# A decoder layer in split fp32: where the weight subtraction and the normalised tiles stand in program order

## The chip, the cores and the metric

The kernel runs on one core of one Trainium2 chip. The number that counts is the device time of one execution in microseconds (us). Before the change it is 1643.07 us, the median of 3 runs (1643.04 to 1643.13).

## The reference

One decoder layer is applied to 256 prompt tokens and 8 x 4 sample tokens, all in fp32. Cut to what matters here:

```python
mod = (silu(c) @ w_ada + b_ada)              # six shifts, scales and gates per conditioning row
h = rms(x, g_mix) * (1 + sc_m) + sh_m
proj = h @ w_in                              # 2048 x 9216, split into b, c, hc, u, v, ga, gb
ya = b * shortconv(c * hc)
yb = gelu(u) * (causal_mix(rms(gelu(v), g_v)) + b_sg)
x = x + gt_m * ((sigmoid(ga) * (ya @ w_pa) + sigmoid(gb) * (yb @ w_pb)) @ w_out)
h2 = rms(x, g_ffn) * (1 + sc_f) + sh_f
x = x + gt_f * ((silu(gate) * up) @ w_ffn_out)   # gate, up = h2 @ w_ffn_in
return rms(x, g_final), conv states, normalised v rows
```

The 288 tokens are the free axis everywhere; features lie on the 128 partitions.

## The kernel before

**Products.** Each 128x128 weight tile is used against 288 tokens once per pass. To keep fp32 accuracy, weights and activations are each split into a high part (rounded to the matmul type fp32r) and a low remainder. One tile product is then a *triple* of matmuls (L238 to L240): high x high, high x low, low x high.

**The split of weights.** A block of weights (1 MB or less) is brought by DMA into one of 7 `raw` buffers. `Blk.split` (L467) takes it in segments of 4 tiles (128x512): ScalarE (ACT in the profile) casts it to `hi` (L479), VectorE (DVE) subtracts to get `lo` (L485). `hi` and `lo` have 4 buffers each, so a cast waits until TensorE (PE) has done the last triple on the segment four before.

**The paced part.** In roughly the first 280 us the order on ACT, DVE and the DMA queue is the order in which the Python code issues the work (PE's order is so throughout). After each triple `feed()` (L247) issues the next segment when no more than `LEAD` (11) tiles are split ahead; cast and subtraction are issued together. When an accumulation in PSUM (`pm`, 4 banks) is complete, its sink copies or adds it into SBUF, an *eviction* (L712 on ACT or L714 on DVE for the unit wA; L735 for the next ones), and `evicted()` (L256) runs one waiting *job*.

**Units.** wA multiplies all 72 column tiles by the first 2 of the 16 k tiles (9 blocks of 16 triples; an eviction after every 2 triples). wB, wX and wC do k tiles 2 to 7 (an eviction after 3 or 6 triples). wD does k tiles 8 to 15 and lies behind the paced part. Blocks of the conditioning product (`ada`: aA, aC, aD, aE) stand between them. wA begins with x not yet normalised (`xe`), so that the sum of squares (`squares1`, L565) can be made meanwhile: its pieces are squares on ACT (L576) and sums on DVE (L579).

**The root.** `root()` (L987) puts three steps into a list of late work: the sums over features (L598) after 16 triples, `diagonal` (L208: L211 and L217 on DVE) 5 triples later, `norm1` (L602) 3 triples later; it multiplies by the diagonal on PE (L223) and copies the result to `rb` (L605).

**The jobs.** `make_h1(k0, k1)` makes the modulated input tiles k0 to k1 in four stages, one tile one stage further at each eviction: `scaled` (L302 on DVE, needs `rb`), `affine` (L617 on ACT, L618 and L619 on DVE, needs the conditioning), `high` (L624 on ACT) and `low` (L630 on DVE). Tiles 2 to 4 are made during wA's block 7, tiles 5 to 7 during wB's last two blocks, each just before the unit that reads them.

Then comes `free` (L995): the remaining jobs are run, the pacing ends, and a scheduler orders ACT, DVE and the DMA queue from there.

Of the kernel before, what the change touches and what calls it, by code (L numbers as in the profile page):

```python
# [22 lines left out]
DFF = 5632  # L23
SLOTS = 92
RAW = 7
LEAD = 11
SEG = 4
SPB = 4
GK = 0.7978845608028654
# [59 lines left out]
def _body(tc, nc, d, pc, pw, pslot, ptmp, pps):  # L89
# [9 lines left out]
    def slot(dt=F32, shape=(P, T)):  # L99
        return pslot.tile(list(shape), dt, tag="s", name=nm("s"), padded_shape=[P, TU])  # L100

    def tmp(n=T):
        return ptmp.tile([P, n], F32, tag="t", name=nm("t"), padded_shape=[P, TU])
# [63 lines left out]
    def token_rstd(ss, n, half=False, gaps=None):  # L167
        got = {}
        V.tensor_tensor(ss.acc, ss.acc, ss.last, ALU.add)

        def fold():
            got["ps"] = psmisc()
            square_sum(got["ps"], ss.acc, True, True)

        steps = [fold, lambda: roots(got, n, half)]
        for f, gap in zip(steps, gaps or (0, 0, 0)):
            if gaps:
                later(f, gap)
            else:
                f()  # L180
        return got
# [26 lines left out]
    def diagonal(got):  # L208
        r = got["r"]
        g = got["diag"] = tmp()  # L210
        V.tensor_tensor(  # L211
            g[:, :TP].rearrange("p (b t) -> p b t", b=2),
            ident.unsqueeze(1).to_broadcast([P, 2, P]),
            r[:, 0:2].unsqueeze(2).to_broadcast([P, 2, P]),
            ALU.mult,
        )
        V.tensor_scalar(g[:, TP:], ident[:, 96:], r[:, 2:3], None, ALU.mult)  # L217
# [26 lines left out]
            feed()  # L244
        return lh

    def feed():  # L247
        while S["feed"] and S["given"] - S["used"] <= LEAD:
            b = S["feed"][0]
            n = len(b.parts or [])  # L250
            b.split(1)
            S["given"] += len(b.parts) - n
            if len(b.parts) == b.nk * b.nm:
                S["feed"].pop(0)
# [10 lines left out]
    jobs = []  # L265
# [3 lines left out]
    def later(f, gap=0):  # L269
        if not pending:  # L270
            since[0] = 0
        pending.append((f, gap))
# [14 lines left out]
    def sam(ap):  # L287
        return ap.rearrange("p (b s) -> p b s", s=NS)

    def bc4(ap):  # L290
        return ap.unsqueeze(2).to_broadcast([P, NB, NS])
# [8 lines left out]
    def normed(kt, rb):  # L300
        t = slot()
        V.tensor_tensor(t, x[:, kt, :], rb, ALU.mult)  # L302
        return t

    def modulate(ks, get, gm, sh0, out):
        hs, his = {}, {}

        def affine(k, t):
            h = tmp()
            hi = slot(F32R)  # L310
            A.activation(
                h[:, :TP], t[:, :TP], AF.Identity, bias=mod[:, sh0 + k, 0:1], scale=gm[:, k, 0:1]
            )
            V.tensor_tensor(sam(h[:, TP:]), sam(t[:, TP:]), bc4(gm[:, k, 1:]), ALU.mult)
            V.tensor_tensor(sam(h[:, TP:]), sam(h[:, TP:]), bc4(mod[:, sh0 + k, 1:]), ALU.add)
            A.copy(hi, h)
            hs[k], his[k] = h, hi

        def finish_(k):
            lo = slot(F32R)  # L320
            V.tensor_tensor(lo, hs[k], his[k].bitcast(F32), ALU.subtract)
            out[k] = (his[k], lo)

        ts = {}
        n = len(ks)
        for i in range(n + 2):
            if i < n:
                ts[i] = get(ks[i])
            if 1 <= i <= n:
                affine(ks[i - 1], ts.pop(i - 1))  # L330
            if i >= 2:
                finish_(ks[i - 2])
# [25 lines left out]
    class Step:  # L358
        defer = False
        raw = None  # L360
        parts = None
# [187 lines left out]
    def ada(name):  # L549
        u = units[name]  # L550
        return [Ada(u, b) for b in range(16 // u[3])]


    S = {}
# [5 lines left out]
    def warm(n, out=None):  # L560
        out = idle if out is None else out
        for _ in range(n):
            PE.matmul(out[:, :T], wb[:, :P], wb, start=True, stop=True)
# [38 lines left out]
    def norm1():  # L602
# [3 lines left out]

        make_h1(0, 2)

    def make_h1(k0, k1):
        made = {}  # L610

        def scaled(k):
            made[k] = normed(k, S["rb1"])

        def affine(k):
            t, h = made[k], tmp()
            A.activation(h[:, :TP], t[:, :TP], AF.Identity, bias=mod[:, k, 0:1], scale=gm1[:, k, 0:1])  # L617
            V.tensor_tensor(sam(h[:, TP:]), sam(t[:, TP:]), bc4(gm1[:, k, 1:]), ALU.mult)  # L618
            V.tensor_tensor(sam(h[:, TP:]), sam(h[:, TP:]), bc4(mod[:, k, 1:]), ALU.add)  # L619
            made[k] = h  # L620

        def high(k):
            hi = slot(F32R)
            A.copy(hi, made[k])  # L624
            made[k] = (made[k], hi)

        def low(k):
            h, hi = made.pop(k)
            lo = slot(F32R)
            V.tensor_tensor(lo, h, hi.bitcast(F32), ALU.subtract)  # L630
            h1[k] = (hi, lo)

        def job(i):
            def f():
                for at, part in enumerate((scaled, affine, high, low)):
                    if k0 <= i - at < k1:
                        part(i - at)

            return f

        jobs.extend(job(i) for i in range(k0, k1 + 3))

    def do_jobs():
        while jobs:
            jobs.pop(0)()
# [38 lines left out]
    def gm_of(k0, k1):  # L684
        V.scalar_tensor_tensor(
            gm1[:, k0:k1, :],
            mod[:, 16 + k0 : 16 + k1, :],
            1.0,
            gmix[:, k0:k1].unsqueeze(2).to_broadcast([P, k1 - k0, NC]),
            ALU.add,  # L690
            ALU.mult,
        )

    def mk_h1(k0, k1):
        def f():
            gm_of(k0, k1)
            if S.get("paced") is not None:
                return make_h1(k0, k1)
            modulate(range(k0, k1), lambda k: normed(k, S["rb1"]), gm1, 0, h1)

        return Do(f)

    part, raws = {}, {}
# [30 lines left out]
    def sinkB(m, ps):  # L734
        return V.tensor_tensor(part[m], ps[:, :T], part[m], ALU.add)  # L735
# [158 lines left out]

    def rstd2():
        S["r2"] = token_rstd(S["acc2"], D, gaps=(9, 0))
        later(lambda: diagonal(S["r2"]), 4)

    def norm2():
        ps = rstd_bcast(S["r2"])  # L900
# [3 lines left out]
    def mk_h2(k0, k1):  # L904
        def f():
            modulate(range(k0, k1), lambda k: normed(k, S["rb2"]), gm2, 48, h2)

        return Do(f)
# [53 lines left out]
    def at(main, plan):  # L962
        out, n = [], 0
        for s in main:
            out.append(s)
            if isinstance(s, Blk):
                n += 1
                out += plan.pop(n, [])
        assert not plan
        return out  # L970

    aA, aC, aD, aE = ada("aA"), ada("aC"), ada("aD"), ada("aE")
# [3 lines left out]
    wB = [Blk("wB", i, rh1, lambda m, ps: sinkB(LATER + m, ps)) for i in range((72 - LATER) // 4)]  # L976
# [7 lines left out]
    steps = [Do(lambda: warm(24)), aA[0], Do(lambda: warm(8)), aA[1], Do(lambda: warm(6)), aA[2], Do(lambda: warm(6)), aA[3]]  # L984
    steps += [Do(mk_xe), Do(lambda: warm(7))]

    def root():  # L987
        later(sums1, 16)
        later(lambda: diagonal(S["r1"]), 5)
        later(norm1, 3)  # L990

    plan = {2: [Do(root, None)], 5: aC[:4], 7: aC[4:] + [mk_h1(2, 5)]}
    steps += at(wA, plan)
    steps += at(wB, {2: aD[:4], 4: aD[4:] + [mk_h1(5, 8)]})
    free = Do(lambda: None, None)  # L995
    steps += at(wX + wC, {3: aE[:4], 8: aE[4:8], 13: aE[8:12], 18: aE[12:] + [free, mk_h1(8, 12), mk_h1(12, 16)]})

# [21 lines left out]
    def ffin(q):  # L1019
        fi = [Blk("fi", i - 4, h2.__getitem__, lambda j, ps: sink_fi(j + 4, ps)) for i in range(max(4, 22 * q), 22 * q + 22)]  # L1020
        return fi
# [3 lines left out]

    fk = [KBlk("fk", i, xg.__getitem__, sink_fk) for i in range(4)]
    nxt = ffin(1)
    steps += [fk[0], Do(norm2, 3), mk_h2(0, 6), fk[1], mk_h2(6, 11), fk[2], mk_h2(11, 16), fk[3]]
    steps += at(ffin(0) + nxt[:2], {2: a5[:4], 6: a5[4:8], 10: a5[8:12], 14: a5[12:]})
    for q in range(3):  # L1030
        steps += ffout(q) + nxt[2:]
# [26 lines left out]
    for s in steps:  # L1058
        if s is free:
            do_jobs()  # L1060
            S["paced"] = None
            head.close()
        if isinstance(s, Do):
            if pending and s.gap is not None:
                later(s.run, s.gap)
            else:
                s.run()
            continue
        i = pos[id(s)]
        if i + AHEAD < len(stream):  # L1070
            stream[i + AHEAD].load()
        while (
            nxt < len(blks)
            and blks[nxt].raw is not None
            and nxt <= cur + 1
            and S["paced"] is None
        ):
            blks[nxt].split()
            nxt += 1
        s.run()  # L1080
        if isinstance(s, Blk):
            cur += 1
            nxt = max(nxt, cur)
# [109 lines left out]
```

## Time and profile before

| what | value |
|---|---|
| median of 3 runs | 1643.07 us |
| the profiled execution | 1643.07 us |
| its span, first to last instruction | 1641.3 us |
| mean granted TensorE clock | 0.998 |
| PE busy | 1625.7 us, 99% of the span |
| DVE busy, ACT busy | 1011.1 us, 738.7 us |

The span is 1.8 us shorter than the time of the same execution. PE is TensorE's matmuls and PEld its weight loads, which run ahead of the matmuls. In a row of the timeline stand the start in us from the span's start, the busy time in us, the engine, the line, the operation, its output and inputs, and in brackets how long the engine was idle before it and what ended that.

### The profile page before, as it was taken

To read this page: it belongs to the slowest core of one execution; us is meant where nothing else is said; L and a number is where in the kernel's file an instruction comes from. 1 tells how busy PE (TensorE), PEld (TensorE's weight loads), DVE (VectorE), ACT (ScalarE), POOL (GpSimd) and SP (SyncE) were. 2 spreads that over 40 slices of the span, in tenths; PEclk is the share of its full clock that TensorE was granted. 3 is DMA by queue.
4 is the path that set the end of the run, shared out by engine and by line. 5 is a ranking of instruction groups with operands and counts; after the bars stand their busy time and mean duration, and the time that the engine had idled before them with its cause. 6 is when DMAs were issued, how large, how long until landed. Compare 5 with 4: busy or idle time off the path is not lost.

```text
span 1641.3 us, 31007 instructions
## 1 busy us (share of the span) xinstructions
PE 1625.7 (99%) x12360; PEld 1550.4 (94%) x12360; DVE 1011.1 (62%) x2162; ACT 738.7 (45%) x1359; POOL 21.7 (1%) x67
## 2 busy tenths in 40 slices
PE   9999999999999999999999999999999999999997
PEld 6889899998998999999998999999999999999997
DVE  5567687877755567667844555555555555555565
ACT  4543344643444334456743434444444444444453
POOL 0000000000000000011000000000000000000000
PEclk9999999999999999999999999999999999999999
DMA  9777775766786767744576546443464434644341
GB/s 366 288 282 288 299 271 201 268 257 261 292 315 257 274 245 289 272 177 154 195 310 249 208 168 206 176 159 122 161 211 175 156 131 159 220 158 169 111 157 58
DMA packets 59425, 357.56 MB, mean 218 GB/s; under 512 B 6640, under 2 KB 9616, under 8 KB 28560
## 3 DMA queue, kind: packets, MB, share of 16 engines
q1 hardware_dynamic: 58992, 355.38, 58.5%
q8 instruction: 96, 1.57, 0.4%
q14 instruction: 49, 0.40, 0.1%
q10 hardware_dynamic: 288, 0.21, 0.0%
HBM read 352.47 MB, written 3.09 MB: 217 GB/s over the span
## 4 chain that ended last, share of the span: by engine, by line
PE 96%; DVE 1%; DMA 1%; ACT 1%; issue 0%; DVEq 0%; ACTq 0%; SPq 0%
PE pm L238 30%; PE pm L239 30%; PE pm L240 30%; PE ada L394 5%; DMA raw<-in_wA 1%; DMA raw<-in_aA 1%; DVE lo L485 0%; ACT hi L479 0%; DVE x L957 0%; DMA ct<-in_c 0%; DVE s L714 0%; PE px L190 0%; PE px L795 0%; PE px L836 0%; DVE s L302 0%
## 5 line engine op out<-in xcount | busy, mean ns | idle before, releaser
L238 PE MATMUL pm<-s,hi 128*128 128x288 f32 (+1 forms) x3760 | 1112.9, 296 | 1.6 <-DVE s L714 1.3
L239 PE MATMUL pm<-s,hi 128*128 128x288 f32 (+1 forms) x3760 | 1110.3, 295 | 1.1 <-DVE s L630 0.7
L240 PE MATMUL pm<-s,lo 128*128 128x288 f32 (+1 forms) x3760 | 1109.7, 295 | 0.2 <-DVE lo L677 0.2
L485 DVE TENSOR_TENSOR lo<-raw,hi 128x512 fp32r<-128x512 f32 (+1 forms) x959 | 654.2, 682 | 497.7 <-ACT hi L479 483.7
L479 ACT CAST hi<-raw 128x512 fp32r<-128x512 f32 (+1 forms) x960 | 588.0, 613 | 801.1 <-PE pm L239 787.1
L238 PEld LDWEIGHTS pm<-s,hi 128*128 128x128 f32 x3760 | 707.1, 188 | 21.9 <-issue 15.9
L239 PEld LDWEIGHTS pm<-s,hi 128*128 128x128 f32 x3760 | 706.8, 188 | 2.2 <-DVE s L630 0.9
L240 PEld LDWEIGHTS pm<-s,lo 128*128 128x128 f32 x3760 | 706.4, 188 | 0.4 <-DVE lo L677 0.4
L394 PE MATMUL ada<-raw,cs 128*32 128x512 f32 (+2 forms) x832 | 88.9, 563 | 1.5 <-DMA raw<-in_aA 1.1
L394 PEld LDWEIGHTS ada<-raw,cs 128*32 128x32 f32 x832 | 23.8, 109 | 48.5 <-issue 43.0
L743 DVE TENSOR_TENSOR s<-pm,s 128x288 f32<-128x288 f32 x72 | 32.9, 457 | 15.9 <-PE pm L240 15.8
L338 DVE SCALAR_TENSOR_TENSOR x<-pm,mod,x 128x256 f32<-128x256 f32 x80 | 38.0, 475 | 2.7 <-PE pm L240 2.7
L297 DVE TENSOR_TENSOR s<-t,s 128x288 fp32r<-128x288 f32 (+1 forms) x76 | 34.7, 459 | 5.9 <-ACT s L295 5.9
L295 ACT CAST s<-t 128x288 fp32r<-128x288 f32 (+1 forms) x76 | 32.6, 433 | 12.4 <-DVE t L775 5.5
L735 DVE TENSOR_TENSOR s<-pm,s 128x288 f32<-128x288 f32 x56 | 25.2, 453 | 7.9 <-PE pm L240 7.8
L922 DVE SCALAR_TENSOR_TENSOR t<-t,pm 128x288 f32<-128x288 f32 x42 | 19.1, 454 | 16.5 <-PE pm L240 16.5
L344 DVE TENSOR_TENSOR t<-pm,mod 128x32 f32<-128x32 f32 x80 | 15.3, 191 | 18.6 <-PE pm L240 18.6
L712 ACT COPY s<-pm 128x298 f32<-128x298 f32 (+1 forms) x42 | 16.9, 403 | 19.7 <-PE pm L240 19.7
L159 ACT ACTIVATE t<-x 128x288 f32<-128x288 f32 (+2 forms) x31 | 13.5, 437 | 20.5 <-DVE x L347 17.4
L720 DVE SCALAR_TENSOR_TENSOR s<-pm,s 128x256 f32<-128x256 f32 x40 | 19.2, 481 | 5.0 <-PE pm L240 5.0
L164 DVE TENSOR_TENSOR acc<-acc,t 128x288 f32<-128x288 f32 x34 | 15.5, 456 | 8.2 <-ACT t L159 8.2
L204 POOL TENSOR_TENSOR r<-e,mhalf 128x3 f32<-128x3 f32 x4 | 4.2, 1040 | 1159.5 <-DVE e L203 1159.5
(134 smaller groups left out, 460.6 us busy)
## 6 DMA issues: line engine op xcount, KB each, us to landing
raw<-in_fi SPq DMA_DIRECT2D x84, 1024.0 KB, 4.8
raw<-in_a SPq DMA_DIRECT2D x64, 1024.0 KB, 9.5
raw<-in_f SPq DMA_DIRECT2D x64, 704.0 KB, 4.1
raw<-in_wD SPq DMA_DIRECT2D x36, 1024.0 KB, 4.9
raw<-in_wC SPq DMA_DIRECT2D x24, 768.0 KB, 4.6
raw<-in_aE SPq DMA_DIRECT2D x16, 1024.0 KB, 10.0
raw<-in_wo SPq DMA_DIRECT2D x16, 1024.0 KB, 4.9
raw<-in_pa SPq DMA_DIRECT2D x8, 1024.0 KB, 5.7
```

Of the source, the lines that this page charges most:

```text
L238: PE.matmul(out, wh, ah, start=first, stop=False)
L239: PE.matmul(out, wh, al, start=False, stop=False)
L240: lh = PE.matmul(out, wl, ah, start=False, stop=last)
L295: A.copy(hi, a)
L297: V.tensor_tensor(lo, a, hi.bitcast(F32), ALU.subtract)
L338: V.scalar_tensor_tensor(x[:, m, :TP], ps[:, :TP], mod[:, gt0 + m, 0:1], x[:, m, :TP], ALU.mult, ALU.add)
L394: PE.matmul(acc[32 * j : 32 * j + 32, :w], cs[:, kt, :], self.raw[:, o : o + w], start=(kt < ks), stop=(kt >= 16 - ks), tile_position=(0, ...
L479: A.copy(hi, self.raw[:, s * 128 : e * 128])
L485: sub()
L720: V.scalar_tensor_tensor(t[:, :TP], ps[:, :TP], t[:, T : T + 1], t[:, :TP], ALU.add, ALU.add)
L735: return V.tensor_tensor(part[m], ps[:, :T], part[m], ALU.add)
L743: V.tensor_tensor(a, ps[:, :T], a, ALU.add)
```

## The change

The subtraction of a segment is issued two triples after its cast instead of together with it (`lows`, `LAG`), and a segment is fed when 12 instead of 11 tiles are ahead, so a cast is issued one triple earlier and its subtraction one triple later than before. The first stage of the jobs (`scaled`) of tiles 2 to 4 and 5 to 7 is issued one block (wA) or one block (wB) earlier by `pre_h1`; `make_h1` then has three stages. The steps of the root stand 6 and 4 triples apart instead of 5 and 3. At the second norm the two gaps change from 4 and 3 to 3 and 4.

```diff
-LEAD = 11
+LEAD = 12
+LAG = 2
...
-    def feed():
+    lows = []
+
+    def feed(force=False):
+        while lows and (force or S["used"] >= lows[0][0]):
+            lows.pop(0)[1]()
         while S["feed"] and S["given"] - S["used"] <= LEAD:
             b = S["feed"][0]
             n = len(b.parts or [])
-            b.split(1)
+            low = []
+            b.split(1, low)
+            lows.append((S["used"] + LAG, low[0]))
...
+    made = {}
+
+    def pre_h1(k0, k1):
+        def scaled(k):
+            def f():
+                made[k] = normed(k, S["rb1"])
+
+            return f
+
+        return Do(lambda: jobs.extend(scaled(k) for k in range(k0, k1)), None)
+
     def make_h1(k0, k1):
-        made = {}
...
-                for at, part in enumerate((scaled, affine, high, low)):
+                for at, part in enumerate(parts):
...
-        jobs.extend(job(i) for i in range(k0, k1 + 3))
+        parts = (affine, high, low) if k0 in made or jobs else (scaled, affine, high, low)
+        jobs.extend(job(i) for i in range(k0, k1 + len(parts) - 1))
...
-        later(lambda: diagonal(S["r2"]), 4)
+        later(lambda: diagonal(S["r2"]), 3)
...
-        later(lambda: diagonal(S["r1"]), 5)
-        later(norm1, 3)
+        later(lambda: diagonal(S["r1"]), 6)
+        later(norm1, 4)
 
-    plan = {2: [Do(root, None)], 5: aC[:4], 7: aC[4:] + [mk_h1(2, 5)]}
+    plan = {2: [Do(root, None)], 5: aC[:4], 6: [pre_h1(2, 5)], 7: aC[4:] + [mk_h1(2, 5)]}
     steps += at(wA, plan)
-    steps += at(wB, {2: aD[:4], 4: aD[4:] + [mk_h1(5, 8)]})
+    steps += at(wB, {2: aD[:4], 3: [pre_h1(5, 8)], 4: aD[4:] + [mk_h1(5, 8)]})
...
-    steps += [fk[0], Do(norm2, 3), mk_h2(0, 6), fk[1], mk_h2(6, 11), fk[2], mk_h2(11, 16), fk[3]]
+    steps += [fk[0], Do(norm2, 4), mk_h2(0, 6), fk[1], mk_h2(6, 11), fk[2], mk_h2(11, 16), fk[3]]
...
             do_jobs()
+            feed(True)
             S["paced"] = None
```

PE executes the same instructions in the same order but for one place, and the DMA queue's order stays. In the changed kernel the same statements have other line numbers: the triple is L239 to L241, the cast L486, the subtraction L252, wA's evictions L730 (ACT) and L732 (DVE), `scaled` L309, `affine` L634 to L636, `high` L641, `low` L647.

The place on PE is the root's product with the diagonal (`px<-t,ones`), in wA's fourth block. Before:

```order
L240 MATMUL pm_119_597<-s_21_236,lo_94_510 128x298
L238 MATMUL pm_119_597<-s_23_242,hi_93_508 128x298
L239 MATMUL pm_119_597<-s_24_244,hi_93_508 128x298
L240 MATMUL pm_119_597<-s_23_242,lo_94_510 128x298
L223 MATMUL px_121_606<-t_117_589,ones_78 128x288
L238 MATMUL pm_123_610<-s_21_236,hi_99_531 128x298
```

And now, with the same names:

```order
L241 MATMUL pm_119_597<-s_23_242,lo_92_503 128x298
L239 MATMUL pm_123_609<-s_21_236,hi_97_524 128x298
L240 MATMUL pm_123_609<-s_22_238,hi_97_524 128x298
L241 MATMUL pm_123_609<-s_21_236,lo_98_526 128x298
L239 MATMUL pm_123_609<-s_23_242,hi_97_524 128x298
L240 MATMUL pm_123_609<-s_24_244,hi_97_524 128x298
L241 MATMUL pm_123_609<-s_23_242,lo_98_526 128x298
L224 MATMUL px_125_619<-t_118_594,ones_78 128x288
```

The product moved behind two more triples. On ACT, at the same place before (`hi` casts of weights from `raw`, evictions `s<-pm`, and the copy of the root `rb<-px`):

```order
L479 CAST hi_109_563<-raw_11_154 128x512
L712 COPY s_113_579<-pm_112_572 128x298
L479 CAST hi_115_585<-raw_13_174 128x512
L712 COPY s_118_595<-pm_114_581 128x298
L712 COPY s_120_604<-pm_119_597 128x298
L605 COPY rb_122_608<-px_121_606 128x288
L479 CAST hi_124_614<-raw_13_174 128x512
L712 COPY s_129_632<-pm_128_625 128x298
```

And now:

```order
L486 CAST hi_103_547<-raw_11_154 128x512
L730 COPY s_105_550<-pm_102_540 128x298
L486 CAST hi_113_579<-raw_13_174 128x512
L730 COPY s_115_582<-pm_112_572 128x298
L730 COPY s_117_592<-pm_116_584 128x298
L486 CAST hi_120_604<-raw_13_174 128x512
L730 COPY s_122_607<-pm_119_597 128x298
L612 COPY rb_126_621<-px_125_619 128x288
```

Each cast moved ahead of the eviction of the accumulation that ends with the triple that frees its buffer, and one cast ahead of the copy of the root. In wA the subtractions on DVE keep their places among the evictions.

On DVE in wA's block 7, from the third `scaled` tile to the eviction of the block's seventh accumulation, before:

```order
L302 TENSOR_TENSOR s_245_1056<-x_77,rb_122_608 128x288
L618 TENSOR_TENSOR t_246_1058<-s_241_1041,gm1_89 128x32
L619 TENSOR_TENSOR t_246_1058<-t_246_1058,mod_88 128x32
L485 TENSOR_TENSOR lo_250_1070<-raw_173_789,hi_249_1068 128x512
L618 TENSOR_TENSOR t_252_1077<-s_245_1056,gm1_89 128x32
L619 TENSOR_TENSOR t_252_1077<-t_252_1077,mod_88 128x32
L630 TENSOR_TENSOR s_254_1083<-t_242_1043,s_247_1062 128x288
L630 TENSOR_TENSOR s_258_1096<-t_246_1058,s_253_1081 128x288
L485 TENSOR_TENSOR lo_261_1104<-raw_173_789,hi_260_1102 128x512
L714 COPY s_262_1109<-pm_259_1098 128x288
L630 TENSOR_TENSOR s_263_1111<-t_252_1077,s_257_1094 128x288
```

And now, to the eviction of the same accumulation (`pm_262`):

```order
L635 TENSOR_TENSOR t_244_1049<-s_208_908,gm1_89 128x32
L636 TENSOR_TENSOR t_244_1049<-t_244_1049,mod_88 128x32
L635 TENSOR_TENSOR t_250_1067<-s_211_920,gm1_89 128x32
L636 TENSOR_TENSOR t_250_1067<-t_250_1067,mod_88 128x32
L647 TENSOR_TENSOR s_252_1073<-t_241_1035,s_245_1053 128x288
L252 TENSOR_TENSOR lo_248_1064<-raw_175_792,hi_247_1062 128x512
L647 TENSOR_TENSOR s_256_1087<-t_244_1049,s_251_1071 128x288
L647 TENSOR_TENSOR s_261_1101<-t_250_1067,s_255_1085 128x288
L252 TENSOR_TENSOR lo_259_1098<-raw_175_792,hi_258_1096 128x512
L732 COPY s_263_1111<-pm_262_1103 128x288
L252 TENSOR_TENSOR lo_266_1122<-raw_175_792,hi_265_1120 128x512
```

The `scaled` tiles are no longer in this stretch (they stand in block 6), and all three `low` stand ahead of that eviction. In wB's last two blocks the same holds on DVE: three `scaled` move from there to the block before, and the third `low` stands one eviction earlier.

## The prediction

> **What bounds the kernel now.** I read the page first: the span, and who is busy in it.
>
> ```profile
> span 1641.3 us, 31007 instructions
> PE 1625.7 (99%) x12360; PEld 1550.4 (94%) x12360; DVE 1011.1 (62%) x2162; ACT 738.7 (45%) x1359; POOL 21.7 (1%) x67
> ```
>
> TensorE sets the time (the page's chain is PE for 96%), and the change neither adds nor removes a matmul. So it can only win what PE waits. The span lies 1.8 us below the execution's 1643.07 us, which is also the median, so what is won in the span comes off 1643.07. Next the windows and the waits of the weight loads, since the order changes only before about 290 us:
>
> ```profile
> 20.00:45.00 25.00, 24.36 (x170) 23.00 (x169) 20.32 (x38) 16.58 (x32) 1.40 (x1) 1.00 0.99 379
> 45.00:132.00 87.00, 85.00 (x674) 76.46 (x672) 56.40 (x129) 43.33 (x92) 0.00 (x0) 1.00 0.75 288
> 132.00:280.00 148.00, 148.00 (x1132) 136.81 (x1131) 111.44 (x288) 55.14 (x92) 0.00 (x0) 1.00 0.71 266
> ...
> PEld pm L238 <- DVE s L714: 2.5, 5, 1.1
> PEld pm L239 <- DVE s L630: 0.9, 1, 0.9
> ```
>
> The columns behind the length are PE, PEld, DVE, ACT and POOL busy, the granted clock (1.00) and the DMA share. PE has no gap at all from 132 to 280; the two wait rows (20 to 132 us), and a third stop at the root, hold nearly all there is to win. The timeline of PE shows the four large stops, each with the matmul before it:
>
> ```profile
> 43.74 0.30 PE L240 MATMUL pm<-s,lo 128*128 128x298 f32 x1
> 44.63 0.75 PE L223 MATMUL px<-t,ones 128*128 128x288 f32 x2 [0.60 <-DVE t L217]
> ...
> 51.65 0.30 PE L240 MATMUL pm<-s,lo 128*128 128x298 f32 x1
> 52.40 0.40 PE L238 MATMUL pm<-s,hi 128*128 128x298 f32 x1 [0.45 <-DVE s L714]
> 52.64 0.30 PE L239 MATMUL pm<-s,hi 128*128 128x298 f32 x1
> 52.77 0.30 PE L240 MATMUL pm<-s,lo 128*128 128x298 f32 x1
> ...
> 83.05 0.29 PE L240 MATMUL pm<-s,lo 128*128 128x288 f32 x1
> 84.22 0.40 PE L238 MATMUL pm<-s,hi 128*128 128x288 f32 x1 [0.88 <-DVE s L714]
> ...
> 125.09 0.30 PE L238 MATMUL pm<-s,hi 128*128 128x288 f32 x1
> 126.05 0.40 PE L239 MATMUL pm<-s,hi 128*128 128x288 f32 x1 [0.67 <-DVE s L630]
> ```
>
> Undisturbed matmuls start 0.13 us apart (52.64 to 52.77), three of them, a triple, take 0.40. After a stop the second start comes 0.24 later (52.40 to 52.64): 0.10 more is lost. Counted from start to start, the stops cost A: 44.63-43.74-0.13 = 0.76 (a matmul of another kind follows, so no 0.10); B: 0.62+0.10 = 0.72; C: 1.04+0.10 = 1.14; D: 0.83+0.10 = 0.93. Together 3.55.
>
> By the brackets of these matmul rows alone the sum would be 0.60+0.45+0.88+0.67 = 2.60, and the time 1640.5. [...]
>
> **The change part by part.** *Gaps of the root (A).* L223 waits for the diagonal:
>
> ```profile
> 42.44 0.41 ACT L712 COPY s<-pm 128x298 f32<-128x298 f32 x1 [1.54 <-PE pm L240]
> 42.74 0.62 ACT L479 CAST hi<-raw 128x512 fp32r<-128x512 f32 x1
> ...
> 43.40 0.69 DVE L485 TENSOR_TENSOR lo<-raw,hi 128x512 fp32r<-128x512 f32 x1 [1.31 <-ACT hi L479]
> ...
> 44.34 0.23 DVE L217 TENSOR_SCALAR t<-cp,r 128x32 f32<-128x32 f32 x1
> ```
>
> A subtraction that waits for its cast stands ahead of the diagonal's two instructions (L211, L217). Now the cast stands ahead of the eviction and starts at 42.44, 0.30 earlier, and all behind it too: L217 ends at 44.27 instead of 44.57. L223 stands two triples (0.41 each at this width, three times 0.137) later, at 43.87+0.82 = 44.69. The second move does it alone but for 0.02; together 0.4 us are spare. A goes: 0.76. The root then comes two triples later for PE, but its first reader, wA's sixth block, is over 20 triples (8 us) away, and the five evictions that run its jobs take 10.
>
> *Casts one triple earlier, subtractions one later (B).* In wA an eviction follows every second triple, so the subtraction keeps its place among evictions; what changes is ACT. B came from this:
>
> ```profile
> 50.62 0.62 ACT L479 CAST hi<-raw 128x512 fp32r<-128x512 f32 x1
> ...
> 51.88 0.46 DVE L714 COPY s<-pm 128x298 f32<-128x298 f32 x1
> ```
>
> The cast stood behind both `high` casts, the eviction behind its subtraction. Now the cast ahead of that eviction (`hi_137`) stands before both. PE stopped at its 73rd triple, undisturbed due at 52.40-0.62 = 51.78; the cast's buffer comes free with the 64th, which ends at 51.78 - 9 x 0.41 + 0.57 = 48.66 (0.27 to its third matmul, 0.30 for it), and 0.76 sooner with A gone: cast 47.9 to 48.6, subtraction about 48.8 (the `affine` halves are first), eviction 49.4 to 49.9. Its bank is wanted at 51.78-0.76 = 51.0. B goes: 0.72, with 1.1 spare.
>
> *`scaled` a block earlier, wA (C).* Before the stop:
>
> ```profile
> 76.95 0.40 ACT L712 COPY s<-pm 128x288 f32<-128x288 f32 x1 [1.42 <-PE pm L240]
> ...
> 81.00 0.60 ACT L617 ACTIVATE t<-s,mod,gm 128x256 f32<-128x256 f32 x1
> 81.51 0.42 ACT L624 CAST s<-t 128x288 fp32r<-128x288 f32 x1
> 81.83 0.39 ACT L712 COPY s<-pm 128x288 f32<-128x288 f32 x1
> ...
> 82.45 0.62 ACT L479 CAST hi<-raw 128x512 fp32r<-128x512 f32 x1
> 82.98 0.39 ACT L712 COPY s<-pm 128x288 f32<-128x288 f32 x1
> ...
> 83.11 0.69 DVE L485 TENSOR_TENSOR lo<-raw,hi 128x512 fp32r<-128x512 f32 x1 [0.51 <-ACT hi L479]
> 83.72 0.45 DVE L714 COPY s<-pm 128x288 f32<-128x288 f32 x1
> ```
>
> Successive starts give what each holds ACT: affine 0.51, `high` 0.32, weight cast 0.52; an eviction 0.29 to 0.30 (42.44 to 42.74). In the times of before, the cast that now stands ahead of the eviction at 76.95 starts there, as both wait for one triple. I walk ACT's new order: eviction 77.47, two affines 77.76 and 78.27, `high` 78.77, cast 79.09, eviction 79.61, affine 79.90, `high` 80.41, eviction 80.73, `high` 81.02, cast 81.34 to 81.96. The subtraction runs from 82.00, the eviction from 82.61 to 83.06 (before: 84.17). The bank is wanted at 83.05+0.13 = 83.18. So C goes, but with 0.1 spare only, and the ACT eviction before it is as close (82.25 against 82.39). For a slip I take 0.10 off: 1.04. The three `scaled` (0.4 each) land in block 6, where DVE has room (56 us busy of the 87 in the windows' second row); if that cover went, they would cost at most their own 1.2.
>
> *The same in wB (D).* The late piece is the third `low`:
>
> ```profile
> 47.36 0.82 DVE L302 TENSOR_TENSOR s<-x,rb 128x288 f32<-128x288 f32 x2
> ...
> 125.55 0.45 DVE L630 TENSOR_TENSOR s<-t,s 128x288 fp32r<-128x288 f32 x1
> ```
>
> It ended at 126.00 and was wanted at 125.22. Two `scaled` take 0.82; three, 1.2, leave the queue ahead of it: 124.8. It is also issued one eviction (1.2 us) earlier. D goes: 0.93.
>
> *The start.* The wait row on L714 counts five: 2.5 less B's 0.62 and C's 1.04 leaves 0.84 for three, all before 32 us, each with 0.10 behind it: about 1.1. There casts wait for weights, and squares stand between them:
>
> ```profile
> 28.16 0.62 ACT L479 CAST hi<-raw 128x512 fp32r<-128x512 f32 x1 [0.98 <-DMA raw<-in_wA]
> ...
> 29.91 1.74 ACT L576 ACTIVATE q<-x 128x1152 f32<-128x1152 f32 x2 [1.13 <-DVE q L579]
> ...
> 32.20 0.69 DVE L485 TENSOR_TENSOR lo<-raw,hi 128x512 fp32r<-128x512 f32 x1 [0.63 <-ACT hi L479]
> ...
> 35.38 0.30 PE L240 MATMUL pm<-s,lo 128*128 128x298 f32 x1
> 35.57 0.41 PE L238 MATMUL pm<-s,hi 128*128 128x298 f32 x1
> ```
>
> An earlier place does not bring weights sooner (DMA share 0.99), and in front of an eviction the waiting cast costs ACT what it gains; I give these three nothing (bounds -0.5, one cast's 0.52 on a late bank, and +1.1). The subtraction at 32.20 gains about 0.55 (an estimate: the second square, half as wide, takes a third of the 1.74, and its cast now stands ahead of it); DVE is without rest behind it, so the small stop at 35.57 (0.19-0.13 = 0.06, and 0.10) goes: 0.2 with rounding.
>
> *Nothing:* the second norm (the gaps sum to 7 as before, and neither PE nor DVE is reordered); `hi` released a triple sooner is wanted 12 triples (4.8 us) on; `raw` held a triple longer delays a DMA issue by 0.4 us, seven steps ahead of use. If that cover went, each late block would cost its delay, 0.4. What PE waits behind `free` stays: there the order is equal.
>
> Sum: 0.76+0.72+1.04+0.93+0.2 = 3.65. 1643.07-3.65 = **1639.4 us**.
>
> **The rivals.** *C and B come back in part* (0.18): the walk left C 0.1 us. If both slip by 0.6 to 1 us, only A, D and half of the rest remain, about 2.5: 1640.6. For it: two evictions at the limit. Against: B has 1.1 spare. *The subtraction keeps its place* (0.10): the edit in words changes nothing on DVE in wA, and with it B and C stay; A and D go, 1.7: 1641.4. Against: the shown ACT order. *The early stops go too* (0.10): 3.65+1.1 = 4.75: 1638.3. For it: ACT casts earlier throughout. Against: the wait for weights.
>
> *Evictions behind casts* (0.05, slower): 33 casts now stand directly ahead of an ACT eviction that is ready at the same moment (before, they stood behind it), each delaying it by 0.52. An eviction ends 0.04+0.41 after its accumulation, and the bank is wanted six triples (2.4 us) after it; the spare 2.0 less 0.52 covers this until ACT is 1.5 us behind. If ACT stays that far behind in its three busy stretches, three evictions each, 9 x 0.52 = 4.7 are lost against 1.7 (A, D) won: 1646.1. [...]
>
> **How the numbers follow.** 0.57 for the forecast; its own range is 1639.0 to 1640.0 (C's slip 0 to 0.5). What this measurement tells from no change is 0.2%, 3.3 us, so the bound lies at 1639.8, inside that range: of the 0.57 some 0.50 lie below. Faster 0.50+0.10 = 0.60, slower 0.05, within 0.35. The range 1638.5 to 1641.5 takes in the forecast, the first two rivals and the near end of the third.
>
> **What would show it.** Right: no wait of L224 for the diagonal; none of `pm` on DVE evictions between 45 and 130 us; none on `low`; the stops before 32 us still there; PE's start-to-start excess in 32 to 130 us down by 3.5. Wrong: new waits of `pm` on L730 (evictions behind casts), or a stop near 82 us of over 0.5.

## The result, and the profile after

The changed kernel takes 1636.85 us (median of 6 runs, 1636.69 to 1637.01); the kernel before takes 1643.18 us beside it (1643.04 to 1643.49). The ratio is 0.9961, with a 95% interval of 0.9948 to 0.9974: 6.3 us are won, where 3.65 had been forecast, and 1636.85 lies below the range (1638.5 to 1641.5). The profiled execution after took 1636.74 us.

The page of the kernel after, its span and who is busy:

```profile
span 1635.0 us, 31014 instructions
PE 1622.2 (99%) x12360; PEld 1548.1 (95%) x12360; DVE 1012.0 (62%) x2162; ACT 739.0 (45%) x1359; POOL 20.8 (1%) x67
```

The same matmuls, 3.5 us less of PE busy time, and a span 6.3 us shorter. The windows after, columns as before:

```profile
20.00:45.00 25.00, 24.91 (x178) 24.11 (x176) 21.20 (x40) 17.27 (x34) 1.23 (x1) 1.00 1.02 392
45.00:132.00 87.00, 87.00 (x698) 79.23 (x697) 59.28 (x135) 44.45 (x93) 0.00 (x0) 1.00 0.76 292
```

PE has no gap left from 45 to 132 us (before: 85.00 of 87.00). Of the weight loads' waits for DVE's evictions in 20 to 132 us (before: 2.5 us in five, and 0.9 for `low`) there remains

```profile
PEld pm L239 <- DVE s L732: 0.5, 2, 0.3
```

and both of these lie before 32 us. At the root, where stop A stood (L212, L218 and L224 are the lines that were L211, L217 and L223), DVE and PE after show:

```profile
43.10 0.42 DVE L212 TENSOR_TENSOR t<-cp,r 128x256 f32<-128x256 f32 x1
43.43 0.24 DVE L218 TENSOR_SCALAR t<-cp,r 128x32 f32<-128x32 f32 x1
...
44.10 0.30 PE L241 MATMUL pm<-s,lo 128*128 128x298 f32 x1
44.24 0.65 PE L224 MATMUL px<-t,ones 128*128 128x288 f32 x2
```

The diagonal is ready at 43.67, the matmul that reads it starts at 44.24, 0.14 behind the one ahead of it: no wait. So the four stops are gone. What the forecast lacks shows in a stretch where no engine's order differs and PE waits for nothing, 800 to 1300 us, first before, then after:

```profile
800.00:1300.00 500.00, 500.00 (x3787) 488.79 (x3786) 271.36 (x520) 214.37 (x378) 0.00 (x0) 1.00 0.54 194
```

```profile
800.00:1300.00 500.00, 500.00 (x3797) 488.81 (x3796) 269.33 (x511) 213.45 (x375) 0.00 (x0) 1.00 0.54 194
```

Both are busy for all 500 us at a granted clock of 1.00, and yet the kernel after starts ten matmuls more, 10 x 0.13 = 1.3 us of work. The matmuls themselves follow each other faster. I call the time from one matmul's start to the next, where nothing waits, the *pitch*. The FFN's first projection shows it best, since there a block is always 16 triples, 48 matmuls, with nothing between. Every second block ends in the tanh that reads its bank (L920 before, L938 after). In the view of that line between 1000 and 1150 us, "a to b" are its first and last start, x11 the count; before, then after:

```profile
L920 ACT ACTIVATE t<-pm x11: 404/405/405, 1017.8 to 1145.1; 128x288 f32<-128x288 f32 x11
```

```profile
L938 ACT ACTIVATE t<-pm x11: 402/403/404, 1012.5 to 1139.2; 128x288 f32<-128x288 f32 x11
```

Ten intervals are 20 blocks: 127.3/20 = 6.365 us before, 126.7/20 = 6.335 after. From the starts of PE's matmuls it is 6.3665 and 6.3337, and the 22 blocks of the second such stage agree with each other to 1 and 2 ns (standard deviation). Three hundredths of a microsecond, in every block.

Where the 6.3 us lie, from the starts of each stage's first matmul in the two traces (positive: won): the first triple starts 0.17 earlier; wA 3.29, wB -0.04, wX 0.90 (stop D), wC -0.24; from wD to the FFN's end 2.23. Split in the other way: for each matmul of a triple I take the time to the next matmul's start, and count as a stop what lies over 0.137 us, where that is more than 0.04. From 32 to 132 us that sum falls from 4.96 to 1.21, by 3.75. That is the forecast's 3.65. From 17 to 300 us it falls by 3.71. With the 0.17 of the start, 6.31 - 3.71 - 0.17 = 2.43 us are left that no stop accounts for: the pitch.

### The profile page after: what moved, and what is told of

The parts are those of the page before. It is cut to its first block, busy times and chain, and to the rows that moved or that the text cites. A ratio compares the mean times of both kernels' runs of the same rounds, so it can differ in the third digit from the quotient of the medians.

```text
span 1635.0 us, 31014 instructions
## 1 busy us (share of the span) xinstructions
PE 1622.2 (99%) x12360; PEld 1548.1 (95%) x12360; DVE 1012.0 (62%) x2162; ACT 739.0 (45%) x1359; POOL 20.8 (1%) x67
## 4 chain that ended last, share of the span: by engine, by line
PE 97%; DMA 1%; DVE 1%; ACT 0%; issue 0%; DVEq 0%; ACTq 0%; SPq 0%
PE pm L239 31%; PE pm L240 30%; PE pm L241 30%; PE ada L401 5%; DMA raw<-in_wA 1%; DMA raw<-in_aA 0%; DMA ct<-in_c 0%; DVE x L975 0%; PE px L191 0%; PE px L813 0%; DVE lo L492 0%; PE px L854 0%; PE px L240 0%; PE px L239 0%; PE px L241 0%
## 5 line engine op out<-in xcount | busy, mean ns | idle before, releaser
L239 PE MATMUL pm<-s,hi 128*128 128x288 f32 (+1 forms) x3760 | 1113.1, 296 | 0.4 <-ACT s L680 0.3
L241 PE MATMUL pm<-s,lo 128*128 128x288 f32 (+1 forms) x3760 | 1108.7, 295 | 0.2 <-DVE lo L695 0.2
L486 ACT CAST hi<-raw 128x512 fp32r<-128x512 f32 (+1 forms) x960 | 588.0, 613 | 818.5 <-PE pm L240 784.1
L492 DVE TENSOR_TENSOR lo<-raw,hi 128x512 fp32r<-128x512 f32 (+1 forms) x849 | 578.6, 682 | 451.3 <-ACT hi L486 438.0
L239 PEld LDWEIGHTS pm<-s,hi 128*128 128x128 f32 x3760 | 706.6, 188 | 19.9 <-issue 15.9
L241 PEld LDWEIGHTS pm<-s,lo 128*128 128x128 f32 x3760 | 707.6, 188 | 0.4 <-DVE lo L695 0.4
L252 DVE TENSOR_TENSOR lo<-raw,hi 128x512 fp32r<-128x512 f32 x110 | 75.5, 688 | 31.5 <-ACT hi L486 30.3
L940 DVE SCALAR_TENSOR_TENSOR t<-t,pm 128x288 f32<-128x288 f32 x42 | 19.1, 454 | 16.0 <-PE pm L241 16.0
L939 DVE SCALAR_TENSOR_TENSOR t<-t,pm 128x288 f32<-128x288 f32 x42 | 18.8, 448 | 0.0
```

The lines of the kernel that those rows point to most:

```text
L239: PE.matmul(out, wh, ah, start=first, stop=False)
L241: lh = PE.matmul(out, wl, ah, start=False, stop=last)
L252: lows.pop(0)[1]()
L486: A.copy(hi, self.raw[:, s * 128 : e * 128])
L492: sub()
```

## Experiments

The placement theory: activation tiles come from a pool of 92 slots of SBUF, and which slot a tile gets depends on the order in which slots are asked for and given back. The change moves such requests (`scaled`, the root, evictions), and behind `free` the same tiles lie at other addresses: by the addresses in the built programs, in the first visit of the FFN's first projection 380 of 960 matmuls read their activation from another slot than before. The theory says that the pitch depends on this layout. Its rival, the timing theory: what arrives earlier at `free` makes DVE, ACT and the transfers meet TensorE in another phase.

**The parts, one at a time.** All are the kernel before with one part of the change. The root's gaps:

```diff
-        later(lambda: diagonal(S["r1"]), 5)
-        later(norm1, 3)
+        later(lambda: diagonal(S["r1"]), 6)
+        later(norm1, 4)
```

> The kernel before with the root's two gaps alone changed (6 and 4 triples in place of 5 and 3). Both theories: stop A goes and B, C, D stay, so 0.76 us are won by 132 us. Placement theory (the 2 us won behind `free` come from other slots of SBUF that the order of allocations hands to the activation tiles): here part of the tiles change their slots too, so the matmul rate behind `free` may move by up to about 1 us either way, in proportion to nothing in the early part. Timing theory (an earlier arrival at `free` lets DVE, ACT and transfers meet TensorE in another phase): the gain behind `free` goes with the early gain, 2.1 x 0.76/4.2 = about 0.4 us. Total 1642.3 by the stops alone.

1641.35 us (ratio 0.9989, 0.998 to 0.9998). The weight loads' waits between 23 and 132 us:

```profile
PEld pm L238 <- DVE s L714: 1.6, 3, 1.1
PEld pm L239 <- DVE s L630: 0.9, 1, 0.9
```

A is gone, C (the 1.1) and D (the 0.9) stay, and B is gone as well, which I had not expected. As I read it, the jobs of the root come later with it and leave that eviction its time; no run parts this further. The profiled execution took 1642.53 us and has a stretch at half clock (0.52, the third number from the right), so its stages are not compared:

```profile
19.50:22.60 3.10, 3.10 (x13) 3.10 (x14) 1.94 (x4) 1.20 (x4) 0.00 (x0) 0.52 1.02 409
```

The `scaled` tiles a block earlier (with `pre_h1` and the list of parts as in the change):

```diff
-    plan = {2: [Do(root, None)], 5: aC[:4], 7: aC[4:] + [mk_h1(2, 5)]}
+    plan = {2: [Do(root, None)], 5: aC[:4], 6: [pre_h1(2, 5)], 7: aC[4:] + [mk_h1(2, 5)]}
...
-    steps += at(wB, {2: aD[:4], 4: aD[4:] + [mk_h1(5, 8)]})
+    steps += at(wB, {2: aD[:4], 3: [pre_h1(5, 8)], 4: aD[4:] + [mk_h1(5, 8)]})
```

> The kernel before with only the `scaled` tiles made one block earlier (pre_h1). Both theories: stops C (1.14) and D (0.93) go, A and B stay: 2.07 won by 132 us, total 1641.1 by the stops alone. If C needs the earlier cast as well (my walk of ACT's order put it in), only D goes: 0.93, total 1642.2. Placement theory: a change behind `free` of up to about 1 us of either sign, not in proportion. Timing theory: about +1.0 behind `free` (2.1 x 2.07/4.2).

1640.36 us (0.9982, 0.9973 to 0.999). The waits that remain between 20 and 132 us are A, B (0.62 of the 1.5) and the early ones:

```profile
PEld pm L238 <- DVE s L725: 1.5, 4, 0.7
PEld px L223 <- DVE t L217: 0.8, 1, 0.8
```

C and D both go without an earlier cast: by the sum of excess over 0.137 the stops from 32 to 132 us fall by 2.16, where 2.07 had been expected. 0.7 us more come from the pitch.

Both constants, and the two halves of that:

```diff
-LEAD = 11
+LEAD = 12
+LAG = 2
...
-            b.split(1)
+            low = []
+            b.split(1, low)
+            lows.append((S["used"] + LAG, low[0]))
```

> The kernel before with only LEAD 12 and LAG 2. By the stops: B (0.72) and the small ones (0.2) go, A shrinks by the 0.30 that the cast stands earlier, C and D stay: 1.2 won by 132 us, total 1641.9. Rival of the prediction (the subtraction keeps its place): B stays, 0.5 won. Placement theory: few tiles have other slots here (20 of 960 matmuls of a first-projection stage), so under 0.3 us change behind `free`. Timing theory: about +0.6 (2.1 x 1.2/4.2).

1635.21 us (0.9952, 0.9939 to 0.9964): faster than the whole change. Of the waits for evictions and jobs from 20 to 132 us only this is left, before 32 us:

```profile
PEld pm L239 <- DVE s L721: 0.5, 2, 0.3
```

All four stops are gone, not B and part of A. And behind wC 2.28 us are won by the pitch, although only 20 of 960 matmuls of a first-projection stage have another slot: my figure for the placement theory (under 0.3) was wrong. One slot in each block of 48 was enough to move that block by 13 ns (6.3665 to 6.3531 us).

> The kernel before with LEAD 12 alone, each subtraction still right behind its cast. It parts the two edits of lead_only, which took all four stops. By the prediction's steps the earlier cast takes B (0.72) and 0.30 of A, and leaves C and D: 1.0 won by 132 us. If the later subtraction is what lets the diagonal, `low` and the DVE evictions through (it stood ahead of each of them), then A, C and D stay nearly whole here and LAG is worth most of the 4 us of lead_only. Behind `free` the layout is another one (60 of 960 matmuls of a first-projection stage), which may move the time by 1 to 2 us either way.

LEAD 12 alone moves a cast and its subtraction together, one triple earlier. It is slower, if anything: 1644.75 us (1.0008, 0.9999 to 1.0017; the profiled execution, the longest of ten, 1646.61). The waits from 20 to 135 us:

```profile
PEld pm L238 <- DVE s L735: 2.7, 1, 2.7
PEld pm L238 <- DVE s L714: 0.9, 3, 0.3
PEld pm L238 <- ACT s L712: 1.5, 2, 0.9
PEld pm L239 <- DVE s L630: 0.9, 1, 0.9
PEld px L223 <- DVE t L217: 0.4, 1, 0.4
```

D stays whole, A keeps 0.31 of its 0.76, B is gone, C falls into two smaller stops (0.48 and 0.27), and two new things appear. One is ACT's evictions, L712, twice: the earlier cast stands ahead of them. That is the prediction's slower rival, at 23.21 (0.86) and at 82.29 (the 0.48). The other is the 2.7 us at 111.60, read from ACT, DVE and PE in turn:

```profile
109.84 1.66 ACT L479 CAST hi<-raw 128x512 fp32r<-128x512 f32 x3 [5.29 <-DMA raw<-in_wB]
...
110.49 0.69 DVE L485 TENSOR_TENSOR lo<-raw,hi 128x512 fp32r<-128x512 f32 x1 [4.85 <-ACT hi L479]
111.10 0.81 DVE L735 TENSOR_TENSOR s<-pm,s 128x288 f32<-128x288 f32 x2
...
108.83 0.29 PE L240 MATMUL pm<-s,lo 128*128 128x288 f32 x1
111.60 0.61 PE L238 MATMUL pm<-s,hi 128*128 128x288 f32 x1 [2.48 <-DVE s L735]
112.00 0.44 PE L239 MATMUL pm<-s,hi 128*128 128x288 f32 x1
112.24 0.44 PE L240 MATMUL pm<-s,lo 128*128 128x288 f32 x1
```

Weights land late, their cast waits, its subtraction waits for the cast, and behind the subtraction stand two evictions whose matmuls had ended by 109.12 (108.83 + 0.29). With LAG 2 the same late weights are there (in lead_only ACT waits 4.70 us for them) and PE does not notice.

> The kernel before with LAG 2 alone (LEAD stays 11): each cast at its old place, its subtraction two triples later in program order. If the subtraction ahead of the diagonal, of `low` and of DVE's evictions is what made A, C and D, they go here and B may stay in part (its cast is not earlier): 2.8 won by 132 us or more, 1640.4 before the layout has its say (1 to 2 us either way). If the earlier cast is what counts (the prediction's step for B and C), B and C stay and 1.7 at most is won.

1635.72 us (0.9953, 0.9939 to 0.9968). The subtraction two triples later is enough by itself: ACT's order is that of the kernel before, instruction for instruction. One wait for a job is left between 20 and 132 us, a third of D:

```profile
PEld pm L240 <- DVE s L637: 0.3, 1, 0.3
```

A, B and C go, and the small stops from 23 to 32 us too, which stay in the changed kernel (0.97 before, 0.89 after): with the cast at its old place wA wins 3.94, with LEAD 12 as well 3.36. In DVE's order of wA, most weight subtractions now stand behind the eviction that used to follow them.

The instruction lists of the four programs, laid side by side, show what wins. lead_only and lead12_only have the same order on ACT, with the earlier casts. On DVE, lead_only has in wA the order of the kernel before but for two places: an eviction in the first block, and one subtraction that moved behind the two instructions of the diagonal. B and C are gone there all the same, so there it is the earlier cast that takes them. lead12_only has the same early casts, but part of its subtractions moved ahead with them, past other work of DVE. What lead_only, lag2_only and the changed kernel share is more time between a cast and its subtraction, won at the one end or at the other. DVE's waits for these casts from 32 to 132 us (us in total, times, longest), in before, lead12_only, lead_only and lag2_only:

```profile
DVE lo L485 <- ACT hi L479: 27.0, 31, 3.8
DVE lo L485 <- ACT hi L479: 22.8, 30, 4.9
DVE lo L252 <- ACT hi L486: 15.7, 20, 3.8
DVE lo L252 <- ACT hi L486: 8.1, 8, 3.7
```

**The slots alone.** Ahead of everything else, one DVE instruction of one column for each of n slots, which are then given back:

```diff
+    spare = [slot() for _ in range(46)]
+    for t in spare:
+        V.memset(t[:, 0:1], 0.0)
+    del spare, t
     mhalf = const("mhalf", [P, 16])
```

This deals the slots anew and leaves every other instruction in its place on its engine.

> The kernel before, with 46 slots of the activation pool taken by a one-column memset on DVE before anything else and given back. Every engine's order is as before but for these 46 memsets, which lie in the wait for the first transfers; half of the matmuls of each stage read their activation from another address. Both theories: A, B, C, D as before. Placement theory: the pitch of the 288-column matmuls shifts, most in the first projection of the FFN, and the time moves by 0.5 to 4 us either way from 1643.2. Timing theory: the same time within 0.3 us, as nothing reaches `free` earlier or later.

1640.03 us (0.9981, 0.9972 to 0.9989): 3.2 us won by nothing but addresses, with A to D in place as before. The control writes the 46 columns to a constant, so that no slot moves:

```diff
+    for _ in range(46):
+        V.memset(ones[:, 0:1], 1.0)
     mhalf = const("mhalf", [P, 16])
```

> The kernel before with 46 one-column memsets on DVE at the same place as in slots_moved_before, but into the constant `ones`, so that every slot stays where it was. Placement theory: 1643.2 within 0.3 us, and a block of the FFN's first projection (16 triples, second visit) takes the 6.366 us that it takes before, to 2 ns. If the memsets' time at the start had made the 3.2 us of slots_moved_before (timing theory), about 1640 here too, and 6.347 us per block.

1643.31 us (ratio 1.0, 0.9991 to 1.0009). The tanh line again, control first, then slots_moved_before:

```profile
L922 ACT ACTIVATE t<-pm x11: 403/405/405, 1017.9 to 1145.2; 128x288 f32<-128x288 f32 x11
```

```profile
L924 ACT ACTIVATE t<-pm x11: 405/407/407, 1016.0 to 1143.0; 128x288 f32<-128x288 f32 x11
```

127.3/20 = 6.365 as before, against 127.0/20 = 6.350 (6.3665 and 6.3466 by PE's starts). In the control every stage from wB to the end takes what it takes before to 0.01 us, but for 0.09 in fk. So the pitch is no chance of an execution: the same layout gave the same time, 6.3665 us per block in both, to a nanosecond.

> The changed kernel with the same 46 slots taken and given back at the start. Every engine's order is that of the changed kernel but for the memsets. Placement theory: no stop A to D comes back, but the rate behind `free` is dealt anew; as the changed kernel's 6.334 us per block of the first projection is the shortest of the six layouts seen, most likely longer, near their mean of 6.35: 0.016 x 84 blocks = 1.3 us slower, 1638.2 (1636 to 1640). If the 2 us behind `free` belong to the change's order: 1636.9 within 0.3.

1637.05 us (0.9961, 0.9946 to 0.9976). The total stands within 0.3, as the rival said, but not for its reason: the FFN's first projection is slower (6.3465 per block, 1.07 us over the four visits, fk among them) and its second faster by 1.42. The layout was dealt anew and the sums happen to meet.

> lead_only (LEAD 12 and LAG 2, the fastest kernel so far, 1635.2) with the same 46 slots taken at the start. In the second and the FFN's first projection its activation tiles have exactly the slots of slots_moved_before. Placement theory: the FFN's first projection takes that kernel's 6.347 us per block, not lead_only's 6.353, although all arrives 4.7 us earlier; stage wB to wC win by the layout what slots_moved_before won there (0.8) and not lead_only's 2.2 less the stops; total 1636 (1634.5 to 1637.5). Timing theory: 6.353 per block and 1635.2 within 0.3.

1635.82 us (0.9954, 0.9938 to 0.9971). A block of the first projection takes 6.3466 us, that of slots_moved_before (6.3466) and not that of lead_only (6.3531), though it comes 4.3 us earlier than in the former. wC and the four visits of each projection win against before exactly what slots_moved_before wins, to 0.01 us: 0.40 in wC, 1.46 and -0.01 in the FFN.

> lead_only with 12 slots taken and given back at the start: a third layout of the same order. Placement theory: the stops of lead_only (none from 32 to 283 us), another pitch; a block of the FFN's first projection somewhere between 6.334 and 6.367 us, the time between 1633 and 1638. Timing theory: 1635.2 within 0.3.

> lead_only with 24 slots taken and given back at the start: a fourth layout of the same order. As for lead_slots_12: 1633 to 1638 by the placement theory, 1635.2 within 0.3 by the other. Either of the two may beat lead_only's 1635.2; if none of the four layouts comes below 1634.5, the layouts seen give no more than that.

1636.81 us (0.996, 0.9945 to 0.9975) and 1637.75 us (0.9967, 0.9954 to 0.9979), at 6.3413 and 6.3405 per block. In neither do the weight loads wait for an eviction or a job from 32 to 132 us. With lead_only and lead_slots_moved these are four layouts of one order of work: 1635.21, 1635.82, 1636.81 and 1637.75, a spread of 2.5 us.

**A forecast from the layout.** LAG 2 and the `scaled` tiles together, all else as before, wait less than any other version. But their tiles in wB, wX and wC have the changed kernel's slots:

> LAG 2 and the `scaled` tiles a block earlier, with LEAD and all gaps as before: no stop from 32 to 283 us, as the 0.30 that lag2_only leaves of D goes too. By the stops alone this is the best version, 1635.7 - 0.3 = 1635.4. Placement theory: its tiles of wB, wX and wC have exactly the slots of the changed kernel (other PSUM banks), so those three stages must go at that kernel's rate: against before they win -0.04 and -0.24 in wB and wC, where lag2_only won 0.56 and 0.85. That is 1.7 us worse than lag2_only, so 1637.1 before the later stages have their say (1636 to 1638), slower than lag2_only though it waits less.

1638.61 us (0.9972, 0.9962 to 0.9982). The weight loads wait for no eviction and no job from 20 to 132 us, and the kernel is 2.9 us slower than lag2_only. The first matmul of wC and of wD, after:

```profile
153.32 0.30 PE L239 MATMUL pm<-s,hi 128*128 128x288 f32 x1
...
279.51 0.29 PE L239 MATMUL pm<-s,hi 128*128 128x288 f32 x1
```

in lag2_scaled:

```profile
153.03 0.30 PE L239 MATMUL pm<-s,hi 128*128 128x288 f32 x1
...
279.22 0.29 PE L239 MATMUL pm<-s,hi 128*128 128x288 f32 x1
```

and in lag2_only:

```profile
152.28 0.30 PE L239 MATMUL pm<-s,hi 128*128 128x288 f32 x1
...
277.37 0.30 PE L239 MATMUL pm<-s,hi 128*128 128x288 f32 x1
```

126.19, 126.19 and 125.09 us for the same 864 matmuls in the same order. wB and wX agree with the kernel after as well (-0.04 and 0.90 against before, in both). The PSUM banks differ between the two while the 126.19 agree, so these two runs show no part of theirs. In the later stages, on which nothing had been forecast, this layout is a poor one: 6.3635 us for a block of the FFN's first projection.

The addresses in the fourteen built programs bear the theory out beyond these pairs. The weights lie at the same addresses in all of them. No version moves a slot that the 384 matmuls of the product with `w_pa` read, and that stage takes 63.67 to 63.69 us in all fourteen. In wC the fourteen range from 125.09 to 126.18 us, but those whose matmuls read the same slots agree to 2 ns: before, root_only and memsets_only (125.94); after and lag2_scaled; lead_only and lag2_only; slots_moved_before and lead_slots_moved (125.54). (The 46 slots move more than the expectation of slots_moved_before says: all of the activation reads of wB, wX and wC, half of those of the FFN's first projection, none of the product with `w_pa`.)

All of it in one table, profiled executions against before's, in us won: "stops" is the fall of the excess from 17 to 300 us as defined above (it would count stretches at half clock too, so root_only and lead12_only are left out), "first" the start of the first triple, "pitch" what remains of the start of the last triple.

| kernel | stops | first | pitch | total | median of the runs |
|---|---|---|---|---|---|
| after | 3.71 | 0.17 | 2.43 | 6.31 | 1636.85 |
| scaled_only | 1.93 | 0.24 | 0.74 | 2.91 | 1640.36 |
| lead_only | 3.64 | 0.03 | 4.18 | 7.85 | 1635.21 |
| lag2_only | 4.28 | 0.19 | 3.22 | 7.69 | 1635.72 |
| lag2_scaled | 4.54 | -0.17 | -0.24 | 4.13 | 1638.61 |
| slots_moved_before | -0.33 | 0.19 | 3.14 | 3.00 | 1640.03 |
| memsets_only | 0.11 | -0.06 | -0.14 | -0.09 | 1643.31 |
| slots_moved_after | 3.66 | -0.06 | 2.44 | 6.04 | 1637.05 |
| lead_slots_moved | 3.94 | -0.12 | 3.52 | 7.34 | 1635.82 |
| lead_slots_12 | 4.23 | -0.28 | 2.62 | 6.57 | 1636.81 |
| lead_slots_24 | 3.92 | -0.05 | 1.47 | 5.34 | 1637.75 |

The stops of a version follow from its order of work: the four layouts of lead_only's order agree to 0.1 us from 32 to 132 us, and the spread of their stops (3.64 to 4.23) lies before that. The pitch runs from -0.2 to 4.2 us without regard to it.

## Why the prediction was right and wrong

*The sum of the stops was right.* 3.65 forecast, 3.75 measured from 32 to 132 us. Of the two counts, 3.55 from start to start and 2.60 by the brackets, the first holds. One term of it does not: A was counted without the 0.10 of the other stops, as a matmul of another kind follows. The traces show that loss there too: from the start of the root's product with the diagonal to that of the next triple went 0.38 us before (44.63 to 45.01) and 0.27 after (44.24 to 44.51). The 3.75 leaves this out, as it counts from the matmuls of triples alone. The early stops stayed, as said (0.97 us before, 0.89 after), D and C went whole, and neither C nor B came back, so the rival of 0.18 is out, and so is that of the subtraction that keeps its place at 1641.4. What had been named as signs came: no wait of L224, none of `pm` on DVE's evictions between 45 and 130 us, none on `low`, and none on L730, the sign of the slower rival.

*The step that failed* is the last sentence of "Nothing": "What PE waits behind `free` stays: there the order is equal." The waits did stay. But the sum took it that equal order and equal waits mean equal time, that is, that a triple costs the same in both kernels. The mean from one matmul's start to the next is 132.51 ns before and 132.26 after, over some 9,200 matmuls of 288 columns behind 300 us: 9,200 x 0.25 ns = 2.3 us. A quarter of a nanosecond was beyond what the quoted rows could show, and it makes two fifths of the gain. "The second norm" and "`hi` and `raw`" on the same list were right: nothing was lost there.

*What each part does was told too simply.* A was given to the root's gaps, B to the earlier cast, C and D to the `scaled` tiles. Each of these does take its stop when it comes alone (root_only, lead12_only and scaled_only). But LAG 2 by itself takes A, B, C and two thirds of D, and beside it the others find little left. The sentence "the subtraction keeps its place among evictions; what changes is ACT" is right for the change in wA: in lead_only B and C go with DVE's order around them as before. What it leaves out is LAG's part in it: LEAD 12 alone, whose subtractions move ahead with the casts, wins nothing (1644.75). The rows that the prediction shows have both ends of the chain, the eviction at 83.72 behind the subtraction at 83.11 behind its cast. An earlier cast loosens it (in lead_only DVE waits 15.7 us for casts where it waited 27.0 before), and so does a later subtraction (8.1 in lag2_only). I took it for an argument about ACT's order alone.

*The slower rival* (evictions behind casts) is real: it shows at 23.21 (0.86 us) and 82.29 (0.48) of lead12_only. In the changed kernel no weight load waits for L730 from 20 to 132 us, so nothing that it costs there shows. The early stops that are back with LEAD 12 and LAG 2 (wA wins 3.36 in lead_only, 3.94 in lag2_only) are waits for DVE's evictions.

*The chances.* Faster by over 0.2% had 0.60 and happened (0.39%). By the stops alone it would have been 0.23%. That the pitch went the same way was luck: nothing had been forecast on it. The range was too narrow below: it held bounds for every term of the sum and none for the constant that the terms were counted with.

A version that beats both kernels is LEAD 12 and LAG 2 without the other edits, 1635.21 us, or LAG 2 alone, 1635.72. Which of the two is better as an order of work is not told by their times: by the stops LAG 2 alone is a little ahead (4.28 against 3.64 to 4.23 in the four layouts of the other), and the layout turns it round.

## What to carry to other kernels

Where an engine takes its instructions in the order of the program (in lead12_only DVE began two evictions at 111.10, behind a subtraction that had waited 4.85 us, though their matmuls had ended by 109.12), put distance between an instruction and the other engine's result that it waits for, so that work that is already able to run stands between. Here it served to issue the subtraction two triples later (4.28 us of stops won in lag2_only), or to issue its cast earlier while the subtraction kept its place (3.64 in lead_only); to move both earlier together won nothing (1644.75 us in lead12_only). Before a difference of a few tenths of a per cent is put down to an order of work, compare the time of one repeated block in a stage that the edit does not touch; if it differs, move the tiles' slots with a few dummy requests and see how far the time goes by that alone.

## What the runs showed of the hardware

The pace of back-to-back matmuls changed in these runs with the places in SBUF from which they read their activations: the 46 slots moved ahead of an unchanged order of work took a block of 48 matmuls of 288 columns from 6.3665 to 6.3466 us. In the fourteen programs such a block took from 6.334 to 6.367 us, 132.0 to 132.6 ns for one matmul and no single figure; in before and after PE is busy from 800 to 1300 us without a gap, at a granted clock of 1.00. In nine of the fourteen the blocks of a stage agree to about 2 ns, in the others to 5 to 15. What in the addresses decides is open. Sorted by the remainder of the address (64 to 4096 bytes) or by the distance between two operands in turn, the pitches fall into no clear classes. It isn't local either: in lead_only one matmul of each 48 reads from another slot, and matmuls ten triples on change their pitch (the first of the fourteenth triple from 135.9 to 133.3 ns).

At a stop of 2.48 us, the one at 111.60 in lead12_only, TensorE's granted clock fell from 1.00 to 0.50. The windows around it, the granted clock third from the right:

```profile
100.00:111.00 11.00, 9.12 (x73) 8.30 (x63) 3.09 (x6) 2.41 (x5) 0.00 (x0) 1.00 0.95 371
111.00:112.00 1.00, 0.40 (x1) 0.40 (x2) 1.00 (x4) 0.49 (x1) 0.00 (x0) 0.55 0.61 252
112.00:115.00 3.00, 3.00 (x17) 2.17 (x20) 2.27 (x5) 0.62 (x1) 0.00 (x0) 0.50 0.05 19
115.00:120.00 5.00, 5.00 (x39) 2.26 (x31) 0.63 (x2) 0.48 (x1) 0.00 (x0) 0.71 0.66 248
```

In the rows shown above, the matmuls start 0.24 apart after the stop (112.00 to 112.24) instead of 0.13. wB lost 5.45 us in all, 2.63 of it by the late start at 111.60 and the rest by the slow matmuls behind it: about twice the length of the stop. It is one case. The stretch at 0.52 in root_only (19.50 to 22.60) had no such stop in the 2.5 us ahead of it, where PE was idle for 0.58 us at most (1.92 busy of 2.50), and what set that one off is open.
